# A hybrid DeltaNet, attention and Conformer trunk on one core: the solver's blocks in fewer stores and more loads, token buffers, and three orders of work

## The chip, the cores and the metric

The kernel runs on one core of one Trainium2 chip. The metric is the device time of one execution in microseconds, as the median of several runs: 1379.72 us for the kernel before, in three runs from 1378.24 to 1382.68 us. A core has five engines with an instruction stream each: TensorE (PE, with its weight loads as PEld), VectorE (DVE), ScalarE (ACT), GpSimd (POOL) and SyncE (SP). In this kernel SP issues nearly all transfers between memory (DRAM) and the on-chip buffers, so SP's stream is one queue of DMA issues.

## The reference

Two layers over 512 latent tokens of width 1024, with 256 context tokens, all in float32. Layer 0 mixes with gated DeltaNet heads in both directions and with attention; layer 1 with a Conformer convolution; a SwiGLU FFN stands behind each. Cut to what matters here:

```python
def reference(x, c, ctx, c_ctx, w_mod, ...):
    h, hc = x, ctx
    for layer in range(2):
        sh1, sc1, gt1, sh2, sc2, gt2 = ada_terms(c, w_mod[layer], b_mod[layer])   # silu(c) @ w_mod + b_mod
        a = rms_norm(h) * (1 + sc1) + sh1
        if layer == 0:
            ac = the same of hc with c_ctx
            y = hybrid_mixer(a, ac, ...)
        else:
            y = conformer_conv(a, ...)
        h = h + gt1 * rms_norm(y)
        f = swiglu_ffn(rms_norm(h) * (1 + sc2) + sh2, w_ffn_in[layer], w_ffn_out[layer])
        h = h + gt2 * rms_norm(f)
    return h

def gated_delta_chunked(q, k, v, g, beta, s0):           # 4 heads of 128, forward and reversed
    decay, kb = ...                                      # in chunks of tokens
    lower = where(strict, (kb @ k.T) * decay, 0)
    u, w = triangular_solve(lower + eye, [v * beta, kb * exp(gcum)])
    for each chunk:                                      # one after the other
        v_new = u - w @ state
        o = q_dec @ state + intra @ v_new
        state = state * exp(g_last) + k_tail.T @ v_new

def attend(q, k, v):                                     # 8 query heads, 2 key heads of 64, 768 keys
    return softmax(q @ k.T / 8) @ v
```

## The kernel before

A float32 product is made of three matmuls: each operand is split in a high and a low part (`whi`, `wlo`; `ah`, `al`), and high x high, high x low and low x high are added (lines 297 to 299, 204 to 206, 1760 to 1762). The split of a weight tile is a cast (`whi`, line 564) and a subtraction (`wlo`, line 573), mostly on DVE.

The program is written by a planner. `Plan.op` collects operations with their engines, costs, dependences and the buffers that they take; `Plan.run` is a list scheduler, which at each step takes from the ready operations the one with the smallest key: its start by the planner's own costs, less a weight times the sum of the longest path behind it and a bias by the operation's name, and, where there is a choice of engines, by its name and engine. The biases are tables of numbers: `BIAS0` for stage 0, `BIAS1` for stage 1, `BIAS` for stage 2, `BIAS2` for the tail. So a table sets both the order on each engine and which engine runs an operation. On the chip each engine works through its list in this order and waits on semaphores where an operand isn't there.

- **Stage 0** (`plan_inputs`). Six token tiles of 128x1024 (four of `xs`, two of `ctx`) are loaded into `xt` (`ld_x`, line 351), squared and summed on ACT (`x_sq`, line 355), brought to a root on POOL (line 180), scaled (`x_norm`, on ACT line 365 or DVE line 367) and transposed on PE (`ps_xt`, line 374) into `xnT`. Beside it the modulation is computed: sixteen weight tiles `mraw` (line 404) are multiplied with the conditioning on PE (`ps_mod`, line 411, four matmuls a tile), turned (line 426) and made into columns; the tokens are then modulated (`a`, line 446), cast to the high part (`aL` for the latent, `aC` for the context tokens) and subtracted to the low part (line 454). The first product of the tokens, keys and values of the attention (`ps_kv`, lines 297 to 299), needs all of these and the split weights `wkhi`, `wklo` (lines 338 and 342). The tiles `xt` have three buffers, `mraw` six.
- **Stage 1** (`plan_heads`). The DeltaNet projections with their short convolution, the gates, and `solver(d)` for the two directions d. The solver inverts the 32x32 unit triangles on the diagonals of the chunks, 4 blocks x 24 (6 chunks x 4 heads) of them, as 96 partitions of 32x32, in 31 steps of row operations on DVE. Its result and the transpose leave for DRAM in `x_out` (line 1110), into `xblk[d]`, from which they are read back in another layout.
- **Stage 2** (`plan_delta` and `plan_attention`). `inverse` builds the inverse of each chunk's triangle of 128 from the 32x32 blocks: `ld_xu` (line 1363) reads a chunk's blocks into `xu` (three buffers), `ld_off` (line 1371) the blocks off the diagonal into `m`, and a chain of small matmuls follows (`ps_w`, `ps_dx`, `ps_du`, line 1334), with copies on DVE, POOL and ACT between them. `step` then carries the state from chunk to chunk (`ps_xr`, `ps_p`, `ps_o`, `ps_ds`). `vt` and `ktl` (lines 1430 and 1444) are loads of values and keys for it. Attention has queries `ps_qt` (line 1213, from `qd`), scores `ps_sc` (lines 1241 and 1242), their exponentials `pr`, transposes `ps_pt` and products `ps_pv`. `ps_qtok` and `ps_qk` are transposed queries and query-key products for the DeltaNet output. Between them run the adaLN products of a later layer part: `wada` tiles of 128x1024 are loaded (line 1624) and multiplied on DVE (`a_dot`, line 1627).
- **Tail** (`plan_tail`). The output projection (`out_proj`, weights `whout`, product `ps_y`), ffn0 (weights `wfin`, product `ps_in`; then `wfout`, product `ps_y`), the Conformer, ffn1, and the rest of the 80 `wada` products. After each `out_proj` a residual is added to `hres`.

The two loops that the change rewrites are these: sixteen stores of 24 partitions in all (two directions, two orientations, four blocks), and twelve loads (two directions, six chunks) of 128 partitions.

```python
for b in range(4):
    SP.dma_start(xblk[d][w, 32 * b : 32 * b + 32].rearrange("r c h q -> (c h) r q"), t_[b * NB : (b + 1) * NB])
...
s["xu"] = scp.tile([P, 2, H, 32], F32, tag="xu", name="xu", bufs=3)
SP.dma_start(s["xu"], xblk[d][:, :, c].rearrange("w p h q -> p w h q"))
```

## Time and profile before

| what | value |
|---|---|
| median of the runs | 1379.72 us (1378.24 to 1382.68) |
| the profiled run, and its span | 1377.72 us, 1375.9 us |
| mean granted clock of PE | 0.992 |
| DMA | 184.76 MB, mean 134 GB/s |
| instructions in the span | 19258 |

The span reaches from the first to the last instruction of the profiled execution; all times of rows below are counted from its start. In a row of the timeline stand the start, the length, the engine, the line, the operation and the shapes, and in brackets the idle time ahead with what ended it. "SPq" is SP's queue of DMA issues: such a row's length is the time that the issue takes, not the transfer. The rows of the stages are shown in the prediction, where they are used.

### The profile page before, as it was taken

The numbers are of one execution on the slowest core, as the hardware profiler recorded it, in microseconds if no ns is written. First come the engines' busy times: TensorE is split into PE (matmuls) and PEld (weight loads), VectorE is DVE, ScalarE is ACT, GpSimd is POOL, SyncE is SP. The second block draws the span as 40 slices with busy tenths as digits, with TensorE's granted clock in tenths as the row PEclk, the third lists the DMA queues.
The fourth block names the chain that finished last, engine by engine and source line by source line (L and its number), as shares of the span: only waits on it lengthen the run. The fifth ranks groups of instructions, "written<-read, shape, count | busy, mean of one in ns | idle before, by whom it ended". The sixth has DMA issues, their size and how long they took to land.

```text
span 1375.9 us, 19258 instructions
## 1 busy us (share of the span) xinstructions
PE 1326.7 (96%) x7343; PEld 1116.3 (81%) x7343; DVE 857.8 (62%) x1625; ACT 453.4 (33%) x983; POOL 256.7 (19%) x347
## 2 busy tenths in 40 slices
PE   5999898999999999999999999999999999999998
PEld 4888797898877888888887878887798888888886
DVE  3588897888888666565667476649663334243223
ACT  6656534877524301111000142114342223222221
POOL 2668563411002300000000011323040000000000
PEclk9999998999999999999999999999999999999999
DMA  8445636641157464545557333201113223233231
GB/s 320 136 147 165 157 116 148 218 143 55 38 203 262 158 200 150 185 160 177 184 202 256 117 103 103 73 28 62 61 65 120 92 92 110 74 122 108 93 105 64
DMA packets 105900, 184.76 MB, mean 134 GB/s; under 512 B 33776, under 2 KB 50496, under 8 KB 105808
## 3 DMA queue, kind: packets, MB, share of 16 engines
q1 hardware_dynamic: 105808, 183.53, 41.3%
q8 instruction: 58, 0.95, 0.3%
q14 instruction: 34, 0.28, 0.1%
HBM read 172.45 MB, written 11.06 MB: 133 GB/s over the span
## 4 chain that ended last, share of the span: by engine, by line
PE 74%; DVE 12%; DMA 7%; issue 2%; ACT 2%; POOL 2%; SPq 1%; DVEq 0%; POOLq 0%; ACTq 0%
PE ps_in L204 12%; PE ps_in L206 12%; PE ps_in L205 12%; PE ps_y L1760 5%; PE ps_y L1762 5%; PE ps_y L1761 5%; DMA wada<-in_wmB 3%; PE ps_in L2114 2%; PE ps_in L2112 2%; PE ps_in L2113 2%; DVE wlo L573 2%; PE ps_pt L1271 2%; DVE cv L653 2%; DVE wada L1627 1%; PE ps_pv L1293 1%
## 5 line engine op out<-in xcount | busy, mean ns | idle before, releaser
L205 PE MATMUL ps_in<-al,whi 128*128 128x512 f32 (+1 forms) x768 | 285.7, 372 | 1.6 <-POOL al L573 1.6
L206 PE MATMUL ps_in<-ah,wlo 128*128 128x512 f32 (+1 forms) x768 | 285.5, 372 | 0.8 <-DVE wlo L573 0.8
L204 PE MATMUL ps_in<-ah,whi 128*128 128x512 f32 (+1 forms) x768 | 285.9, 372 | 0.0
L573 DVE TENSOR_TENSOR wlo<-wraw,whi 128x1024 fp32r<-128x1024 f32 x162 | 204.7, 1265 | 116.4 <-ACT whi L564 109.2
L204 PEld LDWEIGHTS ps_in<-ah,whi 128*128 128x128 f32 x768 | 144.6, 188 | 28.1 <-issue 2.3
L205 PEld LDWEIGHTS ps_in<-al,whi 128*128 128x128 f32 x768 | 144.6, 188 | 27.3 <-POOL al L573 2.3
L206 PEld LDWEIGHTS ps_in<-ah,wlo 128*128 128x128 f32 x768 | 144.6, 188 | 26.7 <-DVE wlo L573 2.1
L180 POOL TENSOR_TENSOR rr<-rr,mhalf 128x1 f32<-128x1 f32 x28 | 17.4, 624 | 790.6 <-DVE rr L1799 765.0
L564 DVE CAST whi<-wraw 128x1024 fp32r<-128x1024 f32 x93 | 64.8, 697 | 158.0 <-PE ps_in L205 108.6
L1760 PE MATMUL ps_y<-whi,hh 128*128 128x512 f32 x352 | 138.0, 392 | 1.8 <-DVE yg L1785 1.8
L1762 PE MATMUL ps_y<-wlo,hh 128*128 128x512 f32 x352 | 137.7, 391 | 0.0
L1761 PE MATMUL ps_y<-whi,hl 128*128 128x512 f32 x352 | 137.6, 391 | 0.0
L1965 ACT ACTIVATE sg<-ps_in 128x512 f32<-128x512 f32 x44 | 26.3, 598 | 302.9 <-PE ps_in L206 302.6
L564 ACT CAST whi<-wraw 128x1024 fp32r<-128x1024 f32 x69 | 72.3, 1049 | 122.7 <-PE ps_y L1761 70.5
L1627 DVE CUSTOM_DVE_ANT_0 wada<-wada,csrow 128x1024 f32<-128x1024 f32 x80 | 97.3, 1231 | 19.7 <-DMA wada<-in_wmB 19.4
L1760 PEld LDWEIGHTS ps_y<-whi,hh 128*128 128x128 f32 x352 | 66.2, 188 | 16.5 <-DVE yg L1785 2.2
L1762 PEld LDWEIGHTS ps_y<-wlo,hh 128*128 128x128 f32 x352 | 66.2, 188 | 14.5
L1761 PEld LDWEIGHTS ps_y<-whi,hl 128*128 128x128 f32 x352 | 66.2, 188 | 14.3
L1781 ACT ACTIVATE junk<-ps_y 128x512 bf16<-128x512 f32 x32 | 19.1, 598 | 137.5 <-PE ps_y L1762 121.0
L1968 DVE TENSOR_TENSOR sg<-sg,ps_in 128x512 f32<-128x512 f32 x44 | 29.1, 682 | 45.5 <-PE ps_in L206 45.5
L653 DVE SCALAR_TENSOR_TENSOR cv<-ps_in,convw,cv 128x510 f32<-128x510 f32 (+3 forms) x80 | 48.9, 639 | 2.6 <-ACT cv L568 1.1
L2112 PE MATMUL ps_in<-whi,ah 128*128 128x512 f32 x128 | 50.0, 391 | 0.0
(390 smaller groups left out, 2584.0 us busy)
## 6 DMA issues: line engine op xcount, KB each, us to landing
wraw<-in_wfin SPq DMA_DIRECT2D x88, 512.0 KB
wada<-in_wmB SPq DMA_DIRECT2D x80, 512.0 KB
wraw<-in_wfout SPq DMA_DIRECT2D x44, 512.0 KB
mraw<-in_wmA SPq DMA_DIRECT2D x16, 512.0 KB
wraw<-in_wcin SPq DMA_DIRECT2D x16, 512.0 KB
wraw<-in_wqkv SPq DMA_DIRECT2D x12, 512.0 KB
wraw<-in_wcout SPq DMA_DIRECT2D x8, 512.0 KB
rw<-grow SPq DMA_DIRECT2D x8, 384.0 KB
```

Source lines behind the costliest of these rows:

```text
L204: E.matmul(ps, wh, xh, start=start, stop=False)
L205: E.matmul(ps, wh, xl, start=False, stop=False)
L206: E.matmul(ps, wl, xh, start=False, stop=stop)
L564: {"ACT": S.copy, "DVE": V.tensor_copy, "Pool": G.tensor_copy}[e](dst, src)
L573: {"DVE": V, "Pool": G}[e].tensor_tensor(dst, a, b, o)
L653: V.scalar_tensor_tensor(s["cv"][:, o], s["ps"][:, i], convw[:, ft, j : j + 1], s["cv"][:, o], op0=ALU.mult, op1=ALU.add)
L1627: V.tensor_tensor_reduce(s["raw"], s["raw"], csrow[0], 1.0, 0.0, ALU.mult, ALU.add, accs[:, part, j : j + 1])
L1760: E.matmul(acc[t], ah[:, ts_], wh[:, o], start=i == 0 and j == 0, stop=False)
L1761: E.matmul(acc[t], al[:, ts_], wh[:, o], start=False, stop=False)
L1762: E.matmul(acc[t], ah[:, ts_], wl[:, o], start=False, stop=end)
L1968: V.tensor_tensor(s["g"], s["g"], pss[1]["ps"], ALU.mult)
L2112: E.matmul(acc[t], k["h"][:, tk], wh[:, o], start=False, stop=False)
```

## The change

Four things are changed.

1. `xt` gets five buffers in place of three and `mraw` four in place of six; the planner counts the first token load 2 us longer.
2. The tensor `xblk` in DRAM has the row within a block as its first dimension, then the block, the chunk and the head: [2, 32, 4, 6, H, 32] in place of [2, 128, 6, H, 32]. `x_out` stores a tile in one transfer of 96 partitions where it took four of 24: 4 stores in all in place of 16. The runs in memory are of 32 numbers (128 bytes) in both.
3. `ld_xu` reads a chunk in four transfers of 32 partitions, one for each block, in place of one of 128: 48 loads in all in place of 12. The planner's costs follow: 0.75 in place of 2.2 for a store of a tile, 4 x 0.47 in place of 0.47 for a load of a chunk.
4. The tables `BIAS0`, `BIAS` and `BIAS2` have new numbers throughout; `BIAS1` and the weights are the same. So stage 0, stage 2 and the tail are put in other orders, while stage 1 keeps its own up to `x_out`, save two small loads on SP that change places.

```diff
-BIAS0, TW0 = {'a_high': 75700, 'a_low': 206192, 'c_silu': -16514, ...
+BIAS0, TW0 = {'a_high': 4187, 'a_low': 281059, 'c_silu': 232311, ...
...
-    xblk = [drp.tile([2, P, 6, H, 32], F32, name=f"xblk{d}") for d in range(2)]
+    xblk = [drp.tile([2, 32, 4, 6, H, 32], F32, name=f"xblk{d}") for d in range(2)]
...
-                    s["x"] = sp.tile([P, D], F32, tag="xt", name="xt", bufs=3)
+                    s["x"] = sp.tile([P, D], F32, tag="xt", name="xt", bufs=5)
...
-                a = last["x"] = op({"SP": 1.47}, ld_x, seq=after("x"), lat=DLAT, take=("xt",))
+                a = last["x"] = op({"SP": 1.47}, ld_x, seq=after("x"), lat=DLAT if "x" in last else DLAT + 2, take=("xt",))
...
-                        w["raw"] = sp.tile([P, 1024], F32, tag="mraw", name="mraw", bufs=6)
+                        w["raw"] = sp.tile([P, 1024], F32, tag="mraw", name="mraw", bufs=4)
...
-        plan = Plan({"a": 6, "r": 2, "xt": 3, "mraw": 6, "wraw": 2, "w": 4, "rows": 2, "a32": 2, "wkr": 2}, BIAS0, TW0, SCALE0)
+        plan = Plan({"a": 6, "r": 2, "xt": 5, "mraw": 4, "wraw": 2, "w": 4, "rows": 2, "a32": 2, "wkr": 2}, BIAS0, TW0, SCALE0)
...
             def x_out(w):
                 def f():
                     t_ = s["xi"] if w == d else s["xj"]
-                    for b in range(4):
-                        SP.dma_start(xblk[d][w, 32 * b : 32 * b + 32].rearrange("r c h q -> (c h) r q"), t_[b * NB : (b + 1) * NB])
+                    SP.dma_start(xblk[d][w].rearrange("r b c h q -> (b c h) r q"), t_[0 : 4 * NB])
...
-            op({"SP": 2.2}, x_out(d), (a,), lat=DLAT)
-            op({"SP": 2.2}, x_out(1 - d), (b,), lat=DLAT)
+            op({"SP": 0.75}, x_out(d), (a,), lat=DLAT + 1)
+            op({"SP": 0.75}, x_out(1 - d), (b,), lat=DLAT + 1)
...
-                SP.dma_start(s["xu"], xblk[d][:, :, c].rearrange("w p h q -> p w h q"))
+                for b in range(4):
+                    SP.dma_start(s["xu"][32 * b : 32 * b + 32], xblk[d][:, :, b, c].rearrange("w r h q -> r w h q"))
...
-            lx = op({"SP": DMA}, ld_xu, seq=after("xu"), lat=DLAT, take=("xu",))
+            lx = op({"SP": 4 * DMA}, ld_xu, seq=after("xu"), lat=DLAT, take=("xu",))
```

Three places of the new order follow. The first is PE at the start of the program, up to the first product of the tokens (`ps_kv`). Before:

```order
L374 MATMUL ps_xt<-masks,xt 128x128 x24
L411 MATMUL ps_mod<-mraw,cz 32x256 x12
L426 MATMUL ps_mod<-quart,rows 128x2 x2
L374 MATMUL ps_xt<-masks,xt 128x128 x12
L411 MATMUL ps_mod<-mraw,cz 32x256 x4
L374 MATMUL ps_xt<-masks,xt 128x128 x4
L426 MATMUL ps_mod<-quart,rows 128x2 x2
L374 MATMUL ps_xt<-masks,xt 128x128 x8
L411 MATMUL ps_mod<-mraw,cz 32x256 x8
L297 MATMUL ps_kv_325<-wkhi,aL_101 128x272
```

With the change PE first has, three times, eight transposes `ps_xt` and four `ps_mod`, and then:

```order
L374 MATMUL ps_xt<-masks,xt 128x128 x8
L426 MATMUL ps_mod<-quart,rows 128x2 x2
L411 MATMUL ps_mod<-mraw,cz 32x256 x4
L374 MATMUL ps_xt<-masks,xt 128x128 x8
L426 MATMUL ps_mod<-quart,rows 128x2 x2
L411 MATMUL ps_mod<-mraw,cz 32x256 x4
L374 MATMUL ps_xt<-masks,xt 128x128 x4
L411 MATMUL ps_mod<-mraw,cz 32x256 x4
L374 MATMUL ps_xt<-masks,xt 128x128 x4
L411 MATMUL ps_mod<-mraw,cz 32x256 x4
L426 MATMUL ps_mod<-quart,rows 128x2 x2
L297 MATMUL ps_kv_333<-wkhi,aL_101 128x272
```

The modulation stands between the transposes in pieces of four, and 32 of its matmuls are ahead of the first `ps_kv`, where 24 were. On ACT the six norms (line 365) now stand between the squares, ahead of the cast `wkhi`; before, all six ran on DVE.

The second place is SP's queue at the border of stages 1 and 2 (`xblk_86` and `xblk_87` are the two directions; `zimg` is a store of the output gate, `csrow` a load). Before:

```order
L1110 DMA xblk_86<-xi 24x32x32 x4
L1142 DMA zimg<-zz 128x256
L1110 DMA xblk_86<-blk 24x32x32 x4
L1110 DMA xblk_87<-blk 24x32x32 x4
L1110 DMA xblk_87<-xi 24x32x32 x4
L1142 DMA zimg<-zz 128x256 x2
L1614 DMA csrow<-csd 128x1024
L1363 DMA xu<-xblk_86 128x2x128
L1363 DMA xu<-xblk_87 128x2x128
L1363 DMA xu<-xblk_86 128x2x128
L1430 DMA vt<-vimg 128x512 x2
L1371 DMA m_2894<-nimg_84 32x4x32 x2
```

With the change:

```order
L1109 DMA xblk_86<-xi 96x32x32
L1109 DMA xblk_86<-blk 96x32x32
L1141 DMA zimg<-zz 128x256
L1109 DMA xblk_87<-blk 96x32x32
L1109 DMA xblk_87<-xi 96x32x32
L1141 DMA zimg<-zz 128x256 x2
L1614 DMA csrow<-csd 128x1024
L1363 DMA xu<-xblk_86 32x2x128 x4
L1363 DMA xu<-xblk_87 32x2x128 x4
L1363 DMA xu<-xblk_86 32x2x128 x4
L1430 DMA vt<-vimg 128x512 x2
L1371 DMA m_2882<-nimg_84 32x4x32 x2
```

The stores are four rows of one transfer, and one of them has passed a `zimg`; the loads of the first three chunks are twelve transfers, in the place of three, ahead of the same `vt` and `m`.

The third place is PE at the first step of `inverse` (the first `ps_w` of each kernel). Before:

```order
L1561 MATMUL ps_qtok<-masks,qs 128x128 x8
L1213 MATMUL ps_qt<-masks,qd 128x128 x2
L1561 MATMUL ps_qtok<-masks,qs 128x128 x4
L1213 MATMUL ps_qt<-masks,qd 128x128 x2
L1334 MATMUL ps_w_3049<-xu,m_2894 64x32 x4
L1561 MATMUL ps_qtok<-masks,qs 128x128 x4
L1334 MATMUL ps_dx<-w_2898,u_2896 32x32 x4
```

With the change:

```order
L1561 MATMUL ps_qtok<-masks,qs 128x128 x4
L1212 MATMUL ps_qt<-masks,qd 128x128 x2
L1561 MATMUL ps_qtok<-masks,qs 128x128 x4
L1240 MATMUL ps_sc<-kst,qh 128x384
L1241 MATMUL ps_sc<-kst,ql 128x384
L1240 MATMUL ps_sc<-kst,qh 128x384
L1241 MATMUL ps_sc<-kst,ql 128x384
L1212 MATMUL ps_qt<-masks,qd 128x128 x6
L1333 MATMUL ps_w_3111<-xu,m_2882 64x32 x4
L1240 MATMUL ps_sc<-kst,qh 128x384
```

The last `ps_qtok` and four score matmuls, which stood behind the first steps of `inverse`, stand ahead of `ps_w`. In the rest of stage 2 attention's pieces are earlier and the steps of the delta chain later. In the tail, six `wada` in place of eight stand among the weights of the output projection, four in place of three go to every four tiles of `wfin`, and SP asks for the last of them with eighteen of ffn0's 22 tiles of `wfout` to come (nine in two lumps among the first four tiles), where eight were left before; the Conformer's matmuls are in another order.

More of the change, by code (lines that the diff above doesn't have):

```diff
@@ L132 @@
 XORD = (0, 1, 2, 3, 4, 5)
[L133 removed]
+BIAS0, TW0 = {'a_high': 4187, 'a_low': 281059, 'c_silu': 232311, 'c_tanh': 40826, 'col': 135122, 'e_ba': 126776, 'e_k': 155419, 'e_v': 228586, 'kv': -6027, 'ld_c': 85019, 'ld_k': -25467, 'ld_late': 33477, 'ld_m': -25475, 'ld_w': 11636, 'ld_x': -23852, 'mod': -40306, 'mods': 118753, 'quarters': 54203, 'rows': 81455, 'turn': -4629, 'w_high': 15179, 'w_low': -332635, 'x_copy': 85335, 'x_eps': 366451, 'x_norm': 27921, 'x_root': 1752, 'x_sq': 107381, 'x_turn': -5686, ('a_high', 'ACT'): 92650, ('a_high', 'DVE'): -546573, ('a_low', 'DVE'): 58817, ('a_low', 'Pool'): 146574, ('e_ba', 'ACT'): 62505, ('e_ba', 'DVE'): 63100, ('e_k', 'ACT'): 129098, ('e_k', 'DVE'): 46060, ('e_v', 'ACT'): -269350, ('e_v', 'DVE'): 12404, ('mod', 'ACT'): 25634, ('mod', 'DVE'): 33866, ('rows', 'ACT'): -100952, ('rows', 'DVE'): 250644, ('w_low', 'DVE'): 430085, ('w_low', 'Pool'): -182664, ('x_copy', 'ACT'): 3255, ('x_copy', 'DVE'): 8749, ('x_norm', 'ACT'): 180579, ('x_norm', 'DVE'): -196162}, 0.000200
```

5 lines of the change are left out of this document (2 added, 3 removed).

## The prediction

> **What bounds the kernel now.** I read the page's busy table and its chain first, then the same counts cut at the stages.
>
> ```profile
> PE 1326.7 (96%) x7343; PEld 1116.3 (81%) x7343; DVE 857.8 (62%) x1625; ACT 453.4 (33%) x983; POOL 256.7 (19%) x347
> PE 74%; DVE 12%; DMA 7%; issue 2%; ACT 2%; POOL 2%; SPq 1%; DVEq 0%; POOLq 0%; ACTq 0%
> ```
>
> PE is busy for 1326.7 of the span's 1375.9 us. The change leaves the matmuls as they are, so what it can win is the 49.2 us in which PE stands still, and time in which PE is busy at a low clock. In the table of windows (us of PE, PEld, DVE, ACT, POOL; then the granted clock, the DMA share, GB/s) the stages are:
>
> ```profile
> 10.00:60.00 50.00, 45.71 (x367) 36.74 (x368) 22.66 (x66) 35.76 (x71) 20.26 (x24) 0.93 0.70 254
> 60.00:226.00 166.00, 155.23 (x1029) 139.57 (x1029) 149.78 (x402) 84.55 (x221) 111.56 (x143) 1.00 0.54 140
> 226.00:394.00 168.00, 162.28 (x1436) 140.22 (x1434) 139.81 (x339) 114.75 (x320) 35.23 (x84) 0.96 0.38 118
> 394.00:700.00 306.00, 302.02 (x1412) 249.57 (x1413) 206.46 (x293) 50.55 (x101) 23.30 (x24) 1.00 0.56 188
> 700.00:1000.00 300.00, 292.56 (x1386) 242.36 (x1385) 197.63 (x348) 69.97 (x133) 46.51 (x46) 1.00 0.33 111
> 1000.00:1375.90 375.90, 368.94 (x1718) 307.86 (x1717) 140.22 (x173) 94.61 (x136) 19.14 (x24) 1.00 0.28 96
> ```
>
> The first 10 us hold no matmul. Between 10 and 60 PE loses 4.3 us, in stage 1 10.8 (DVE, at 149.78 of 166, is nearly as full as PE there), in stage 2 5.7, then 4.0, 7.4 and 7.0. The clock is below 1.00 in two stages only, the first and stage 2. So the gains to look for are the start, the border of stages 1 and 2, and small holes behind it.
>
> **Stage 0: five token buffers and a new order.** Rows of SP, of ACT and of PE, one group with its mean duration, and two pieces of the chain:
>
> ```profile
> 2.59 1.38 SPq L351 DMA_DIRECT2D xt<-in_xs  x3
> 12.92 0.33 SPq L351 DMA_DIRECT2D xt<-in_xs  x1
> 14.63 1.28 SPq L351 DMA_DIRECT2D xt<-in_ctx  x2
> ...
> 8.11 1.06 ACT L355 ACTIVATE sq<-xt 128x1024 bf16<-128x1024 f32 x1 [5.54 <-DMA xt<-in_xs]
> 9.07 0.19 ACT L355 ACTIVATION_READ_ACCUMULATOR sq<-xt 128x1 f32 x1
> 19.12 1.06 ACT L355 ACTIVATE sq<-xt 128x1024 bf16<-128x1024 f32 x1 [1.42 <-DMA xt<-in_ctx]
> 22.09 0.81 ACT L446 ACTIVATE a<-xnT,cols 128x512 f32<-128x512 f32 x1
> 22.94 0.62 ACT L314 CAST aL<-a 128x512 fp32r<-128x512 f32 x1
> 23.94 1.10 ACT L338 CAST wkhi<-wkr 128x1088 fp32r<-128x1088 f32 x1
> 25.20 0.58 ACT L314 COPY xnT<-ps_xt 128x512 f32<-128x512 f32 x1 [0.16 <-PE ps_xt L374]
> ...
> 28.88 0.39 PE L297 MATMUL ps_kv<-wkhi,aL 128*128 128x272 f32 x1
> L367 DVE TENSOR_SCALAR xt<-xt,ssq_in 128x1024 f32<-128x1024 f32 x6 | 4.5, 752 | 2.4 <-POOL ssq_in L180 2.3
> 20.54 0.56 POOL ssq_in L180
> 30.66 0.57 PE ps_mod L411 x8
> ```
>
> Before, the fourth token tile is asked for at 12.92, when a buffer is free, and the fifth and sixth at 14.63; the last but one reaches ACT at 19.12. With five buffers SP asks for five tiles in a row, so a fourth and fifth come behind the third at the pace of the first ones, and loading binds no more. What is late next is ACT: the order gives it all six norms, which ran on DVE at 752 ns each. The nearest row for such a pass on ACT is the square of the same 128x1024 tile, 1.06 us. ACT then has six squares of 1.06 + 0.19 and six norms of about 1.06, 13.9 us from 8.11 on, so to 22.0; the last norm waits for its root (0.56 on POOL, with DVE's step ahead of it about 1.1), to 23.1. Behind it stand, on ACT, wkhi 1.10, a copy 0.58, the modulation 0.81 and the cast 0.62: 26.2. So the first kv matmul (L297) can start at about 26.2 in place of 28.88, 2.7 us earlier, and two more groups of modulation matmuls are done by then, 2 x 0.57 = 1.1 us. Against this: PE works in shorter pieces from 11 to 26, and its clock, 0.93 in the mean of this stage before, may be low when the kv matmuls begin, or the smaller ring of four mraw buffers may hold modulation back. I take -2.3 us, from -3.8 (all of it) to +2.7 (the kv start gains nothing and 5.4 us of kv run at half clock). Stage 1 keeps its order and its loads (DMA share 0.54), so an earlier start passes through it.
>
> **The solver's blocks.** SP's rows, the last piece of the way out, the copy that makes the last tile, the return, and four windows:
>
> ```profile
> 207.52 3.02 SPq L1110 DMA_DIRECT2D xblk<-xi  x4
> 211.48 6.07 SPq L1110 DMA_DIRECT2D xblk<-blk  x8
> 217.65 3.10 SPq L1110 DMA_DIRECT2D xblk<-xi  x4
> 220.85 2.17 SPq L1142 DMA_DIRECT2D zimg<-zz  x2
> 223.55 2.08 SPq L1363 DMA_DIRECT2D xu<-xblk  x3
> 226.66 3.19 SPq L1371 DMA_DIRECT2D m<-nimg  x6
> ...
> 219.74 4.94 DMA xblk<-xi
> 212.04 1.05 ACT L564 COPY xi<-ps_x 96x512 f32<-96x512 f32 x2
> L1363 SPq DMA_DIRECT2D xu<-xblk x12: 360/374/464, 223.5 to 337.6; - x12
> 230.70 1.03 PE ps_w L1334 x8
> 236.80 0.32 PE ps_sc L1241
> ...
> 207.50:217.50 10.00, 10.00 (x74) 9.38 (x72) 8.19 (x17) 3.98 (x8) 4.23 (x12) 1.00 0.75 125
> 224.00:230.00 6.00, 2.60 (x17) 1.73 (x16) 5.01 (x15) 4.42 (x24) 2.30 (x8) 0.97 0.84 254
> 230.00:243.00 13.00, 12.30 (x90) 10.20 (x91) 7.15 (x17) 3.56 (x15) 2.29 (x9) 0.50 0.46 128
> 372.40:383.20 10.80, 10.50 (x110) 9.44 (x109) 7.77 (x15) 6.99 (x23) 0.84 (x1) 1.00 0.46 145
> ```
>
> The way out: sixteen transfers hold SP for 3.02 + 6.07 + 3.10 = 12.2 us; the last tile is ready at 213.1 and starts to leave at 217.65, because SP is behind; all has landed at 219.74 + 4.94 = 224.7. Four transfers take SP some 3 us at the 0.76 us of one such issue (6.07 / 8), so the last starts at 213.1. The bytes and the 128-byte runs stay the same in number. While these transfers run the DMA engines are busy for just 0.75: if that idle quarter is used, 17.2 us (207.5 to 224.7) become 12.9, and all lands at 220.4; if not, at 224.7 as before. I take 222, between the two, as nothing here shows a 96-partition transfer of such runs.
>
> The return: twelve loads become 48, 36 more issues at 0.374 us, 13.5 us of SP in all. Nine of these stand ahead of the first step, since three chunks' loads precede the vt and m loads, and each pushes them by about 0.4. If all has landed at 222: zimg (2.17) and csrow leave by 220.8, four pieces of the first chunk by 222.4, eight more by 225.7, two vt by 226.6, six m by 229.8. Before, the last m was issued by 226.66 + 3.19 = 229.85: what the way out wins the return spends, and the first ps_w stays at 230.7. If nothing lands earlier, it slips by 6 x 0.4 = 2.4 us. The other 27 extra issues fall on a queue with room between its loads and cost nothing unless a chunk's m or ktl loads come late.
>
> [...]
>
> What does help is the new order on PE. From 224 to 230 PE works 2.60 of 6 us. The change puts four score matmuls (0.32 us each at 236.80, at half clock: 1.3 us) and the last ps_qtok ahead of the first ps_w, some 2 us of work for that hole. I take -2.0 us for the border, with -3.4 (the whole hole) and +2.4 (the slip) as ends, the clock apart. The clock falls to 0.50 after this hole and stays there for 13 us with PE busy 12.30; half of that, 6.2 us, is its price. A hole half as long might spare it; I take it that it doesn't.
>
> [...]
>
> **The rest of stage 2 and the tail.** Attention is moved ahead and the delta steps back; PE is near full in 226 to 394, so I take 0, with 3 us to either side (half of its 5.7 us of holes). In the tail:
>
> ```profile
> 390.00:460.00 70.00, 64.37 (x334) 52.67 (x334) 59.31 (x94) 22.04 (x54) 17.52 (x19) 1.00 0.64 226
> 740.00:760.00 20.00, 18.17 (x81) 14.66 (x80) 15.31 (x23) 2.75 (x8) 0.00 (x0) 1.00 0.68 226
> 745.16 1.23 DVE L1627 CUSTOM_DVE_ANT_0 wada<-wada,csrow 128x1024 f32<-128x1024 f32 x1 [2.52 <-DMA wada<-in_wmB]
> ```
>
> At 745 DVE waits 2.52 us for a wada load, with the split of the next weights and the ps_y products queued behind it, and PE loses 1.83 of 20 us. The new order puts more wada products beside ffn0's wfin, where PE is dense, and has them all behind it when eighteen wfout tiles are left: -1.8 us, with +1.8 as the other end, since nine loads in two lumps ahead of the early wfout tiles can bring the same wait there. In 390 to 460 PE loses 5.6 us of 70 around out_proj; fewer wada there, -0.8 (0 to -2). The conformer's order is new on a DVE that fills a good part of that stage: 0, with 2 us to either side.
>
> **Sum.** -2.3 - 2.0 - 0.8 - 1.8 = -6.9 us. The profiled run took 1377.72, which makes 1370.8; the median shown is 1379.72, 2.0 us above it, so the forecast in its terms is **1372.8**. A measurement of this kernel tells about 0.3%, 4.1 us, from no change.
>
> **The rivals.**
>
> *The gains at the front go in waits.* Stage 1's DVE sets the pace, the kv phase starts cold, the blocks land no earlier. For it: DVE at 149.78 of 166, and the 2.4 us of the return. Against: ACT's sum, which frees 2.7 us. Only the tail's 1.8 us stay: 1377.9.
>
> *The clock holds.* With the holes at 11 to 26 and at 224 to 230 filled, neither low stretch comes: the forecast less 6.2 us and about 1 us of kv, 1365.6. For it: the hole's 3.4 us shrink to some 1.4. Against: all of ps_qt, ps_qtok and the scores hang on DVE's qd copies, and DVE is at 5.01 of 6 there.
>
> *Slower: the delta chain stands bare at the end of stage 2.* The return is late and attention goes first, so the last chunk's chain has nothing beside it. Its price: a chunk's chain, w to o, fills 372.4 to 383.2, 10.8 us with PE at 10.50, some 4 of them attention's; those become idle, and a hole of that kind brought 0.50 clock for 13 us, 6.2 more. That is +10.2 - 2.3 - 2.6 for stage 0 and the tail, with the border at 0: 1385.0. It decides when PE idles over 3 us in one piece before out_proj. Against: attention work still stands in the last rows of stage 2 in the new order.
>
> **How the numbers follow.** The forecast, 1368 to 1378, gets 0.50; the gains lost at the front 0.20; the clock that holds 0.15; the bare chain 0.15. Faster by over 0.3% is under 1375.6: all of the held clock and 0.42 of the forecast, 0.57. Within 0.3%: 0.08 of the forecast and the lost gains, 0.28. Slower: the bare chain, 0.15. The range leaves out the bare chain beyond its lower edge, some 0.12, and the deepest part of the held clock, 0.05: 1362 to 1384. The likeliest case's own is 1368 to 1378.
>
> **What would show it.** Right: the first ps_kv near 26.2 with six norms on ACT; the last block landing near 222, and the first ps_w within a us of where it stood relative to stage 1's end; a fuller PE in the 6 us ahead of it; no loss in wfout. Wrong: ps_kv not before 28.9; a clock of 0.50 in the kv matmuls, or none after the border; a hole over 3 us before out_proj; holes in the conformer beyond those of before.

## The result, and the profile after

| | median of 15 runs | range | profiled run | its span |
|---|---|---|---|---|
| before | 1377.67 us | 1371.0 to 1382.68 us | 1377.72 us | 1375.9 us |
| after | 1382.73 us | 1379.66 to 1387.49 us | 1384.46 us | 1382.7 us |

One run of the changed kernel, of 1459.26 us, and two of middle_new below, of 2934.78 and 3379.62 us, were disturbed and are left out. The changed kernel is slower: the ratio of its time to that of before is 1.0043, with a 95% interval of 1.0031 to 1.0054, so +5.9 us (4.3 to 7.4); the medians of the table differ by 5.1. The prediction was 1372.8 us with a range of 1362 to 1384; the time lies within the range, on the side that had a chance of 0.15.

The page of the changed kernel, its PE row and its chain by engine:

```profile
PE 1330.1 (96%) x7343; PEld 1115.2 (81%) x7343; DVE 866.6 (63%) x1634; ACT 448.9 (32%) x971; POOL 263.7 (19%) x350
...
PE 66%; DVE 16%; DMA 9%; ACT 3%; POOL 2%; issue 2%; SPq 1%; DVEq 0%; POOLq 0%; ACTq 0%
```

PE's share of the chain fell from 74% to 66%, DVE's rose from 12% to 16%: the chain to the end now runs over DVE more often. The windows of the same kernel (us of the window, then of PE, PEld, DVE, ACT, POOL; granted clock, DMA share, GB/s), with the edges used before, and three short ones:

```profile
10.00:60.00 50.00, 46.89 (x374) 36.41 (x375) 29.76 (x81) 30.69 (x61) 20.25 (x23) 1.00 0.72 254
60.00:226.00 166.00, 155.76 (x1025) 141.04 (x1023) 148.31 (x399) 84.04 (x217) 111.66 (x144) 0.98 0.53 142
226.00:394.00 168.00, 161.03 (x1433) 137.66 (x1432) 139.60 (x338) 116.69 (x325) 30.99 (x80) 0.98 0.41 123
394.00:700.00 306.00, 300.77 (x1403) 246.95 (x1403) 216.20 (x315) 50.80 (x101) 21.36 (x24) 1.00 0.62 202
700.00:1000.00 300.00, 290.43 (x1362) 239.61 (x1361) 185.98 (x313) 65.98 (x124) 58.88 (x50) 0.99 0.27 93
740.00:760.00 20.00, 20.00 (x90) 16.51 (x89) 10.06 (x12) 2.76 (x8) 0.00 (x0) 1.00 0.25 84
950.00:960.00 10.00, 6.14 (x34) 5.46 (x33) 9.99 (x20) 4.59 (x9) 4.69 (x2) 0.83 0.32 107
224.00:230.00 6.00, 3.95 (x25) 2.79 (x25) 5.81 (x19) 4.77 (x26) 1.15 (x4) 1.00 0.40 109
230.00:236.00 6.00, 4.27 (x37) 3.06 (x35) 4.71 (x12) 4.97 (x13) 4.44 (x7) 0.96 0.62 162
236.00:243.00 7.00, 7.00 (x42) 5.56 (x42) 2.79 (x6) 4.00 (x10) 1.18 (x5) 0.55 0.33 103
1000.00:1382.70 382.70, 375.20 (x1753) 313.47 (x1752) 145.03 (x184) 97.22 (x141) 19.81 (x26) 1.00 0.28 94
```

Between 10 and 60 the clock is 1.00 where it was 0.93, and PE does 1.2 us more work. From 700 to 1000 PE loses 9.6 us where it lost 7.4, and POOL's work there grew from 46.51 to 58.88 us. The worst ten microseconds are 950 to 960: PE at 6.14 of 10.

Fixed windows slide over the work when two kernels are shifted against each other. So I also cut each kernel's own trace at matmuls that all of them have. This table is worked out from the first and last start of such groups (us; kv is `ps_kv`, z `ps_z` of stage 1, w the first `ps_w`, mix the last product of stage 2, then the first product of the output projection, of ffn0's two products, and of the Conformer's input and output products):

```
               kv starts  to end of z   z to w  w to mix  projection  ffn0 in  ffn0 out  Conformer, in to out  out
before         28.9       27.6+160.4    13.8    160.6     49.7        250.9    124.9     134.1 (125.7+8.4)     52.2
after          27.5       27.4+160.9    16.4    158.7     49.8        252.2    124.5     139.0 (121.6+17.4)    52.1
tail_old       26.8       28.0+158.8    17.3    157.2     49.3        252.4    124.8     134.1 (125.6+8.5)     52.2
tail_new       29.3       28.5+160.8    13.6    159.2     50.5        253.8    123.7     138.8 (121.5+17.3)    52.2
stage0_new     26.7       28.7+159.9    13.9    162.3     51.1        254.2    124.9     134.1 (125.7+8.4)     52.4
wlo_dve2       26.7       30.8+160.6    17.6    156.1     50.4        253.4    125.3     133.6 (121.6+12.0)    53.5
wlo_dve8       26.9       27.9+158.6    17.6    157.7     49.5        254.2    123.9     130.5 (118.0+12.5)    54.6
blocks_new     27.4       27.6+159.1    15.5    161.8     49.5        252.3    127.1     134.1 (125.7+8.4)     52.3
middle_new     28.1       28.5+159.2    17.3    158.6     49.8        251.3    124.2     134.1 (125.7+8.4)     52.2
loads4_only    29.4       28.5+158.8    16.5    162.1     48.5        251.4    123.4     134.1 (125.6+8.5)     52.2
m_first        26.5       27.7+160.8    12.1    190.8     50.9        250.8    125.5     134.1 (125.6+8.5)     52.3
blocks_held    27.8       27.6+157.7    12.6    164.3     49.6        255.1    124.0     134.1 (125.6+8.5)     52.7
best_a         27.2       27.0+159.2    13.7    159.2     50.3        251.2    124.6     129.8 (122.7+7.1)     53.3
best_d         27.2       27.6+159.2    12.0    165.6     50.6        252.3    123.9     129.7 (122.6+7.1)     53.5
after_fix      26.5       28.3+159.4    17.2    159.1     51.5        254.3    124.8     130.8 (118.4+12.4)    54.8
```

The rows below the first two are the experiments (best_b and best_c are left out). The Conformer's column repeats to 0.1 us in kernels that share its code: 134.1 with the old table (seven rows besides before), 138.8 and 139.0 with the new one. Most other columns scatter by 2 to 4 us between profiled runs of the same code (ffn0 in: 250.8 to 255.1 with the old table). So a change of 4.9 us in the Conformer can be read from single profiles, and most of the rest needs the timed comparisons. Of these 4.9 us, the input products take 4.1 less, and the stretch from the last of them to the first output product takes 9.0 more (17.4 in place of 8.4).

**The Conformer.** The timeline of the changed kernel at its worst place, DVE, POOL and PE (`xtok` are the tokens that PE turns into `ps_a` for the next product):

```profile
948.95 6.02 DVE L2350 TENSOR_SCALAR xtok<-xtok,mv 128x512 f32<-128x512 f32 x4
...
949.86 4.83 POOL L573 TENSOR_TENSOR wlo<-wraw,whi 128x1024 fp32r<-128x1024 f32 x2
...
952.54 0.66 PE L1832 MATMUL ps_a<-masks,xtok 128*128 128x128 f32 x4 [2.02 <-DVE xtok L2350]
955.02 0.94 PE L1832 MATMUL ps_a<-masks,xtok 128*128 128x128 f32 x6 [1.83 <-DVE xtok L2350]
```

and the row of that tile, with least, median and greatest ns, of the changed kernel:

```profile
L2350 DVE TENSOR_SCALAR xtok<-xtok,mv x8: 537/542/2565, 948.9 to 969.8; 128x512 f32<-128x512 f32 x8
```

and of the kernel before:

```profile
L2350 DVE TENSOR_SCALAR xtok<-xtok,mv x8: 539/542/954, 945.6 to 964.8; 128x512 f32<-128x512 f32 x8
```

The same instruction takes 0.54 us alone and up to 2.57 us while POOL subtracts two weight tiles (`wlo`, 4.83 us for both) beside it. Four of them fill 6.02 us where four at 0.54 are 2.2, and PE stands still for 2.02 and 1.83 us in between. PE is also slower behind the second hole: the starts of thirteen of its 128x256 matmuls reach over 2.56 us, from 955.98 to 958.54, and over 1.41 (947.33 to 948.74) in wlo_dve8, an experiment below without these holes. In the trace of before the like was there, but PE waited less for it; its timeline has

```profile
931.27 2.78 DVE L573 TENSOR_TENSOR spl<-spa,sph 128x512 fp32r<-128x512 f32 x1
...
930.97 2.53 POOL L573 TENSOR_TENSOR wlo<-wraw,whi 128x1024 fp32r<-128x1024 f32 x1 [0.78 <-ACT whi L564]
```

where the same `spl` takes 0.68 us alone. What PE waited for these two tiles in the whole run (total, times, longest), before:

```profile
PE ps_y L2286 <- DVE spl L573: 1.4, 1, 1.4
PE ps_a L1832 <- DVE xtok L2350: 0.3, 1, 0.3
```

and in the changed kernel:

```profile
PE ps_a L1832 <- DVE xtok L2350: 3.9, 2, 2.0
PE ps_y L2286 <- DVE spl L573: 2.1, 3, 1.1
```

**The border of stages 1 and 2.** SP's rows of the changed kernel:

```profile
207.25 0.32 SPq L1109 DMA_DIRECT2D xblk<-xi  x1
207.67 2.90 SPq L1109 DMA_DIRECT2D xblk<-blk  x1
210.66 2.89 SPq L1141 DMA_DIRECT2D zimg<-zz  x1
213.64 0.38 SPq L1109 DMA_DIRECT2D xblk<-blk  x1
214.12 2.99 SPq L1109 DMA_DIRECT2D xblk<-xi  x1
217.20 3.35 SPq L1141 DMA_DIRECT2D zimg<-zz  x2
220.64 0.41 SPq L1614 DMA_DIRECT2D csrow<-csd  x1
221.14 6.46 SPq L1363 DMA_DIRECT2D xu<-xblk  x12
227.64 0.90 SPq L1430 DMA_DIRECT2D vt<-vimg  x2
228.59 3.20 SPq L1371 DMA_DIRECT2D m<-nimg  x6
```

The return starts 2.4 us earlier than before (221.14 against 223.55), but its first twelve issues take 6.46 us where three took 2.08, so `m` is issued by 231.79 where it was by 229.85, though stage 1 ended 1.1 us sooner. The blocks did land earlier: packets under 512 bytes, nearly all of them the blocks' runs of 128, pass at 440 to 620 in each half microsecond from 217.0 to 220.5 and have ended by 222.0; before, they passed at 390 to 550 up to 222.0, and the last landed at 224.7. The first `ps_w` comes 16.4 us behind stage 1 in place of 13.8. PE's rows ahead of it:

```profile
230.94 0.56 PE L1212 MATMUL ps_qt<-masks,qd 128*128 128x128 f32 x2 [0.36 <-POOL qd L564]
231.68 0.56 PE L1212 MATMUL ps_qt<-masks,qd 128*128 128x128 f32 x2 [0.18 <-POOL qd L564]
232.24 0.62 PE L1333 MATMUL ps_w<-xu,m 128*64 128x32 f32 x8
```

Here it follows `ps_qt` at once, with no wait for a transfer; before, it waited 1.1 us for `m`.

**Stage 0.** ACT and PE of the changed kernel:

```profile
19.83 1.06 ACT L355 ACTIVATE sq<-xt 128x1024 bf16<-128x1024 f32 x1 [1.20 <-DMA xt<-in_ctx]
21.83 1.15 ACT L365 ACTIVATE xt<-xt,ssq_in 128x1024 f32<-128x1024 f32 x1 [0.85 <-POOL ssq_in L180]
22.88 1.08 ACT L338 CAST wkhi<-wkr 128x1088 fp32r<-128x1088 f32 x1
...
25.24 0.62 ACT L314 CAST aL<-a 128x512 fp32r<-128x512 f32 x1
...
25.87 0.66 PE L374 MATMUL ps_xt<-masks,xt 128*128 128x128 f32 x4
26.45 0.64 PE L411 MATMUL ps_mod<-mraw,cz 128*32 128x256 f32 x8
27.02 0.61 PE L426 MATMUL ps_mod<-quart,rows 128*128 128x2 f32 x4
27.49 0.37 PE L297 MATMUL ps_kv<-wkhi,aL 128*128 128x272 f32 x1
```

The last norm ends at 22.98 (the sum had 23.1), though ACT waited 1.20 us for the last token tile, and the cast that `ps_kv` needs ends at 25.86 (26.2 in the sum). Then PE has transposes and modulation left ahead of `ps_kv`, until 27.49.

### The profile page after: what moved, and what is told of

The parts are those of the page before. It is cut to its first block, busy times and chain, and to the rows that moved or that the text cites. A ratio compares the mean times of both kernels' runs of the same rounds, so it can differ in the third digit from the quotient of the medians.

```text
span 1382.7 us, 19354 instructions
## 1 busy us (share of the span) xinstructions
PE 1330.1 (96%) x7343; PEld 1115.2 (81%) x7343; DVE 866.6 (63%) x1634; ACT 448.9 (32%) x971; POOL 263.7 (19%) x350
## 4 chain that ended last, share of the span: by engine, by line
PE 66%; DVE 16%; DMA 9%; ACT 3%; POOL 2%; issue 2%; SPq 1%; DVEq 0%; POOLq 0%; ACTq 0%
PE ps_in L206 9%; PE ps_in L204 9%; PE ps_in L205 9%; PE ps_y L1762 6%; PE ps_y L1760 6%; PE ps_y L1761 6%; DMA wada<-in_wmB 4%; DVE wlo L573 3%; DMA wraw<-in_wfin 2%; PE ps_in L2112 2%; PE ps_in L2114 2%; PE ps_in L2113 2%; DVE wada L1627 2%; DVE cv L653 1%; DVE whi L564 1%
## 5 line engine op out<-in xcount | busy, mean ns | idle before, releaser
L573 DVE TENSOR_TENSOR wlo<-wraw,whi 128x1024 fp32r<-128x1024 f32 x159 | 196.2, 1235 | 113.7 <-ACT whi L564 106.6
L573 POOL TENSOR_TENSOR matsl<-fraw,matsh 128x512 fp32r<-128x512 f32 x5 | 8.1, 1644 | 319.4 <-ACT matsh L564 319.4
L573 POOL TENSOR_TENSOR wlo<-wraw,whi 128x1024 fp32r<-128x1024 f32 x22 | 54.1, 2462 | 47.3 <-DVE whi L564 25.8
```

Of the source, the lines that this page charges most:

```text
L573: {"DVE": V, "Pool": G}[e].tensor_tensor(dst, a, b, o)
```

## The experiments

All fifteen were timed in up to five rounds, each beside the kernel before on the same chip, mostly twelve runs of each (eleven of tail_old, ten of middle_new, five of m_first, four of best_b and best_c); ratios are to it, with 95% intervals, and 0.1% is 1.4 us. The theory from this profile: the loss is the new order of the tail, by POOL's subtractions beside DVE's work in the Conformer. The rivals: the loss is the return of the blocks; or it is spread, and stage 0's gain was never there.

**tail_old.** The changed kernel with the tail's table of before.

```diff
-BIAS2, TW2 = (the table of after)
+BIAS2, TW2 = (the table of before)
```

> The changed kernel with the tail's table of before; stages 0 to 2 stay as changed. Theory A (the loss lies in the tail's new order, above all in the Conformer): from out_proj's start to the end it takes what it took before, so the span falls from 1382.7 to about 1376, and the time is that of the kernel before within 0.2%. Rival B (the loss comes from the front, from the blocks or attention's order): it stays within 1 us of the changed kernel, about 0.4% slower than before.

Ratio 0.9995 (0.9982 to 1.0007), median 1377.12 us. The loss is gone with the tail's table, and so is the pair of POOL's subtractions at 950: the Conformer takes 134.1 us.

**tail_new.** The reverse: the kernel before with the new tail's table alone.

```diff
-BIAS2, TW2 = (the table of before)
+BIAS2, TW2 = (the table of after)
```

> The kernel before with the tail's new table alone. Theory A: about 6 us slower than before (+0.4%), with 139 us in place of 134 from the first Conformer input product to the first output product. Rival B: within 1 us of before.

Ratio 1.0037 (1.0022 to 1.0052): +5.1 us (3.0 to 7.2), nearly all of the change's +5.9. The Conformer takes 138.8 us, 4.7 more. Its window from 880 to 960 against that of tail_old; tail_new first:

```profile
880.00:960.00 80.00, 73.87 (x387) 62.36 (x386) 56.79 (x93) 20.65 (x34) 29.94 (x21) 0.98 0.19 60
```

and tail_old:

```profile
880.00:960.00 80.00, 76.83 (x414) 65.50 (x413) 50.65 (x90) 21.69 (x38) 21.08 (x17) 1.00 0.16 53
```

The new order has 8.9 us more POOL work there and DVE is busy 6.1 us longer, for three instructions more; PE loses 3.0 us more and the clock dips to 0.98. (The Conformer begins 3.5 us later in tail_new, so the two windows aren't quite over the same work.)

**stage0_new.** The kernel before with the first stage of the change (five `xt`, four `mraw`, the first load counted longer, its table).

```diff
-s["x"] = sp.tile([P, D], F32, tag="xt", name="xt", bufs=3)
+s["x"] = sp.tile([P, D], F32, tag="xt", name="xt", bufs=5)
...
-w["raw"] = sp.tile([P, 1024], F32, tag="mraw", name="mraw", bufs=6)
+w["raw"] = sp.tile([P, 1024], F32, tag="mraw", name="mraw", bufs=4)
...
-BIAS0, TW0 = (the table of before)
+BIAS0, TW0 = (the table of after)
```

> The kernel before with stage 0's new table and buffers alone. If the 1.6 us by which the last ps_kv is earlier passes through stage 1 and 2, it is 1.5 us faster than before (0.1%); the prediction had 2.3. If stage 1 or the border takes it back, no change.

Ratio 0.9985 (0.9970 to 1.0000), so -2.1 us (-4.1 to 0.0), and `ps_kv` starts at 26.7. The gain is about there, though the interval touches one. The start of `ps_kv` scatters: 26.5 to 27.5 in the profiles of the table with the new stage 0, 26.5 to 29.4 in those with the old one.

**wlo_dve2.** The changed kernel with two of the Conformer's subtractions `wlo` emitted on DVE in place of POOL: the pair at 949.86, and nothing else. The order on all engines is otherwise kept.

```diff
+            conf = ph[0] == "2"
...
+                if conf and e == "Pool":
+                    n_low.append(e)
+                    if len(n_low) in (7, 8):
+                        e = "DVE"
                 tt_on(e, s["l"], s["raw"], f32(s["h"]), ALU.subtract)
```

> The changed kernel with two operations moved: the two subtractions of the Conformer's output weights (wlo, 128x1024) that ran on POOL at 949.9 to 954.7 stand on DVE behind the four scalings xtok and the splits of a. Theory C (POOL's work beside them stretched the four xtok from 2.2 to 6.0 us, and PE waited 3.9 us for them): the four xtok take 2.2 us again, PE's two holes before ps_a go, and the span falls by 2 to 3 us, as the subtractions now take 2.4 us of DVE ahead of the first output products. Rival D (the order leaves too little PE work beside this chain, whoever runs the subtractions): the holes stay or move behind the splits, and the span changes by less than 1 us.

Ratio 1.0014 (1.0000 to 1.0027), so 0.29% or 4.0 us less than the change (some 1.5 to 6.5 by the two intervals). The tile's row and the window of this kernel (its lines are seven further down):

```profile
L2357 DVE TENSOR_SCALAR xtok<-xtok,mv x8: 539/541/546, 952.4 to 969.5; 128x512 f32<-128x512 f32 x8
```

```profile
950.00:960.00 10.00, 9.90 (x73) 8.95 (x71) 9.47 (x30) 7.80 (x13) 1.42 (x2) 1.00 0.04 14
```

No `xtok` is above 0.55 us, PE works 9.90 of 10, and the stretch ahead of the output products falls from 17.4 to 12.0 us, while those products take 1.4 longer: -5.4 + 1.4 = -4.0. DVE took over work from POOL and the kernel got faster: it is the overlap that costs, not the amount of DVE work.

**wlo_dve8.** All eight of the Conformer's POOL subtractions on DVE.

```diff
-                    if len(n_low) in (7, 8):
+                    if len(n_low) in (1, 2, 3, 4, 5, 6, 7, 8):
```

> The changed kernel with all eight of the Conformer's wlo subtractions that were planned on POOL put on DVE where they were issued. Theory C (POOL's work beside DVE's stretches DVE): beside what the last two gave (4 us), the three holes of 2.1 us at 883 to 899 go, at a cost of six times 1.2 us of DVE where DVE has room; from the first Conformer input product to the first output product it takes 131 to 133 us, against 139 of the changed kernel and 133.6 with two moved. Rival D (DVE's load is what counts): more than 134 us.

Ratio 1.0007 (0.9991 to 1.0024), the Conformer 130.5 us and its output products 54.6. Against wlo_dve2 that is 3.1 us less in the one and 1.1 more in the other, and the ratio is 0.0007 or 1.0 us lower; by the intervals the six others aren't told from nothing.

**blocks_new.** The kernel before with the new layout, the stores and the loads alone; the planner's costs and all tables as before, so that the order stays.

```diff
-for b in range(4):
-    SP.dma_start(xblk[d][w, 32 * b : 32 * b + 32].rearrange("r c h q -> (c h) r q"), t_[b * NB : (b + 1) * NB])
+SP.dma_start(xblk[d][w].rearrange("r b c h q -> (b c h) r q"), t_[0 : 4 * NB])
...
-SP.dma_start(s["xu"], xblk[d][:, :, c].rearrange("w p h q -> p w h q"))
+for b in range(4):
+    SP.dma_start(s["xu"][32 * b : 32 * b + 32], xblk[d][:, :, b, c].rearrange("w r h q -> r w h q"))
```

> The kernel before with the new layout of xblk alone: four stores of 96 partitions, 48 loads of 32, with the planner's costs and all tables of before, so that nothing else changes its place. Theory E (what the merged stores win, the nine more load issues ahead of vt and m spend, and more): from the last ps_z to the first ps_w it takes 16 to 17 us in place of 13.8, and since PE has less to do there in the old order, the time rises by 1 to 3 us (0.1 to 0.2%). Rival F (the stores' earlier landing carries): 13 us or less, and 1 to 2 us faster.

Ratio 1.0024 (1.0009 to 1.0038): +3.3 us. In its waits of PE (total, times, longest) stands

```profile
PE ps_w L1333 <- DMA m<-nimg: 4.1, 1, 4.1
```

where before had one wait of 1.1 us: the first step waits for `m`, which stands behind the return's issues, and comes 15.5 us behind stage 1 (16 to 17 were expected).

**middle_new.** The same with the planner's new costs and the new table of stage 2.

```diff
+op({"SP": 0.75}, x_out(d), (a,), lat=DLAT + 1)
...
+lx = op({"SP": 4 * DMA}, ld_xu, seq=after("xu"), lat=DLAT, take=("xu",))
...
+BIAS, TW = (the table of after)
```

> The kernel before with the blocks' layout, their planner costs and stage 2's new table; stage 0 and the tail as before. The prediction had -2.0 us for this. From the sum of the runs so far (old tail -0.7, stage 0 alone -2.1) it should be 1 us slower than before (+0.1%): ps_w 2.5 us later, made up by the scores ahead of it, and nothing gained. If attention's order is worth its -2.0, 1376.5.

Ratio 1.0013 (0.9996 to 1.0031): +1.8 us. Attention's new order may win back 1.5 of the blocks' 3.3; the intervals overlap, so that isn't shown. The three parts alone add up to -2.1 + 1.8 + 5.1 = +4.8, beside +5.9 (4.3 to 7.4) together: they don't depend on each other in a way that can be seen.

**loads4_only.** The kernel before with the old layout and its sixteen stores, but four loads a chunk.

```diff
-SP.dma_start(s["xu"], xblk[d][:, :, c].rearrange("w p h q -> p w h q"))
+for b in range(4):
+    SP.dma_start(s["xu"][32 * b : 32 * b + 32], xblk[d][:, 32 * b : 32 * b + 32, c].rearrange("w r h q -> r w h q"))
```

> The kernel before with the loads of a chunk in four pieces of 32 partitions (48 loads), and with the stores, the layout and all tables of before. Theory E (the loads' issues on SP, nine more ahead of the first m, make the border late): the stores end as before, the first ps_w comes 3.5 to 4 us later than before after the last ps_z (17 to 18 us in place of 13.8), and the kernel is 3 to 5 us slower. Rival G (what the blocks alone lost, 3.3 us, came from the stores or the new layout): within 1 us of before.

Ratio 1.0036 (1.0024 to 1.0048): +5.0 us for the loads alone, so the new stores may win some 1.7 (5.0 - 3.3), which the intervals don't tell from nothing. Three of its rows on SP:

```profile
223.08 5.61 SPq L1364 DMA_DIRECT2D xu<-xblk  x12
228.74 0.90 SPq L1431 DMA_DIRECT2D vt<-vimg  x2
229.68 3.19 SPq L1372 DMA_DIRECT2D m<-nimg  x6
```

The twelve issues take 3.5 us more than the three of before, and `m` is out by 232.87, 3.0 later. The first `ps_w` moved by 2.7, and waits 4.4 us for `m`.

**m_first.** blocks_new with the loads of `m` ahead of the blocks' loads, by a dependence in the planner.

```diff
-lx = op({"SP": DMA}, ld_xu, seq=after("xu"), lat=DLAT, take=("xu",))
 l1 = op({"SP": 2 * DMA}, ld_off(m1, 32), after(("m1", d)), lat=DLAT)
 l2 = op({"SP": DMA}, ld_off(m2, 64), after(("m2", d)), lat=DLAT)
+lx = op({"SP": DMA}, ld_xu, seq=after("xu") + ((l1, l2) if i == 0 else ()), lat=DLAT, take=("xu",))
```

> The blocks alone (stores of 96 partitions, 48 loads) on the kernel before, with the loads of m for the first chunk of each direction asked for ahead of that chunk's blocks; the planner puts both vt there too, and sets some of stage 2 anew behind it. Theory E: m no longer waits behind twelve issues; the first ps_w comes 11 to 13 us after the last ps_z, in place of 15.5 with the blocks alone and 13.8 before, and the 3.3 us that the blocks alone lost are won back, 0 to 2 us under before. Rival G: first ps_w and time as with the blocks alone, 0.2% slower.

Ratio 1.0205 (1.0187 to 1.0224). The first `ps_w` came 12.1 us behind stage 1, 3.4 sooner than in blocks_new, but the rest of stage 2 took 190.8 us in place of 161.8: with one dependence more, the list scheduler laid the whole stage in another order. This tells nothing of the loads.

**best_b and best_c.** The same dependence, with stage 0 of the change and all of the Conformer's subtractions on DVE; best_b has the new blocks, best_c the old ones. The lines beside those of wlo_dve8 and stage0_new are:

```diff
+lx = op({"SP": DMA}, ld_xu, seq=after("xu") + ((l1, l2) if i == 0 else ()), lat=DLAT, take=("xu",))
```

> Stage 0's new table and buffers, the Conformer's subtractions on DVE, the blocks' new layout and the m loads ahead of it, all on the kernel before with its tables for stage 2 and the tail. If the parts add up: 3.7 us of the first two and 0 to 2 of the last, 1372 to 1374, 0.3 to 0.4% under before. If m ahead of the loads gives nothing, about 1377.

> As the one before, but with the blocks' layout, stores and loads of before: m ahead of three loads in place of twelve. By theory E the first m is issued 1.2 us earlier at most, and the blocks land as late as before (the last store started at 217.65), so the border is the same within 1 us: 1373 to 1375, 0.25% under before. If this is faster than the one with the new layout, the new layout has no use even with m ahead.

Ratios 1.0160 (1.0139 to 1.0181) and 1.0182 (1.0158 to 1.0207): the same spoilt order (191.1 and 188.3 us from the first `ps_w` to the end of stage 2), so no answer.

**blocks_held.** blocks_new with the planner left alone, and only SP's issues shifted as they are written out: the loads of the third chunk and both `vt` are held back until the first `m` are out.

```diff
+                def out(t=s["xu"]):
                     for b in range(4):
-                        SP.dma_start(s["xu"][32 * b : 32 * b + 32], xblk[d][:, :, b, c].rearrange("w r h q -> r w h q"))
+                        SP.dma_start(t[32 * b : 32 * b + 32], xblk[d][:, :, b, c].rearrange("w r h q -> r w h q"))
+                seen[0] += 1
+                held.append(out) if seen[0] in (3,) else out()
...
+                    seen[1] += 1
+                    while seen[1] >= 4 and held:
+                        held.pop(0)()
...
+                held.append(out) if seen[1] < 4 else out()
```

> The blocks alone (stores of 96 partitions, 48 loads) on the kernel before; on SP the six m loads now stand behind the first two chunks' loads, and the third chunk's four loads and both vt behind them. All other engines keep the order of the blocks alone. Theory E: the first m is issued 2.7 us earlier, the first ps_w comes 12 to 13 us after the last ps_z (15.5 with the blocks alone, 13.8 before), and the time falls by 2 to 4 us, to that of before within 1 us. Rival G (the layout or the stores cost the time): 15 us and 0.2% slower, as with the blocks alone.

Ratio 0.9990 (0.9975 to 1.0004); the interval lies below that of blocks_new. SP's rows:

```profile
219.45 3.68 SPq L1365 DMA_DIRECT2D xu<-xblk  x8
223.17 3.18 SPq L1376 DMA_DIRECT2D m<-nimg  x6
226.39 2.02 SPq L1365 DMA_DIRECT2D xu<-xblk  x4
```

`m` is out at 226.35, and the first `ps_w` comes 12.6 us behind stage 1. So the loss of blocks_new, in the old order of PE, was the queue ahead of `m`. Even then the new blocks don't gain measurably over before. The two profiles alone wouldn't have shown the difference: from stage 1's end to the end of stage 2 they have 176.9 and 177.3 us, and in that of blocks_held the clock was at half from 224 to 243.

**best_a.** The kernel before with stage 0 of the change, as in stage0_new, and all of the Conformer's POOL subtractions (five in this order) on DVE.

```diff
+BIAS0, TW0 = (the table of after)
...
+                if conf and e == "Pool":
+                    n_low.append(e)
+                    if len(n_low) in (1, 2, 3, 4, 5, 6, 7, 8, 9, 10, 11, 12, 13, 14, 15, 16, 17, 18, 19):
+                        e = "DVE"
```

> The kernel before with stage 0's new table and buffers, and with the Conformer's five wlo subtractions that ran on POOL put on DVE where they were issued. Stage 0 gives 2.1 us. In the Conformer of before DVE's spl took 2.8 us where 0.7 is usual, beside two such subtractions (931 to 936), and PE lost 1.4 us to it: by theory C 1 to 2 us more, about 1375 in all; by rival D no more than stage 0's 2.1 us, or less, since DVE is full there.

Ratio 0.9973 (0.9958 to 0.9989), median 1376.02 us: 3.7 us faster than before (1.5 to 5.8). The Conformer takes 129.8 us in place of 134.1 and its output products 53.3 in place of 52.2.

**best_d.** best_a with the blocks of blocks_held.

```diff
+held.append(out) if seen[0] in (3,) else out()
```

> Stage 0's new table and buffers, the Conformer's subtractions on DVE, and the blocks with m ahead as in blocks_held, with the tables of before for stage 2 and the tail. If the parts add: 3.7 us and what blocks_held shows, so 1373 to 1375, 0.25 to 0.4% under before.

Ratio 0.9973 (0.9955 to 0.9990): no better than best_a, so the new blocks add nothing that these runs can tell where `m` isn't held up.

**after_fix.** The changed kernel with wlo_dve8 and SP's order of blocks_held.

```diff
+                    if len(n_low) in (1, 2, 3, 4, 5, 6, 7, 8):
...
+held.append(out) if seen[0] in (3,) else out()
```

> The changed kernel with both causes taken away: the Conformer's eight subtractions of POOL on DVE, and on SP the first m loads ahead of the third chunk's loads and of vt. The first alone gave 1.0007 of before. If the queue on SP is the rest: the first ps_w 13 to 14 us after the last ps_z in place of 16.4, and 1 to 3 us less, 0.998 to 1.000 of before. If not: 1.0007 again.

Ratio 0.9996 (0.9978 to 1.0014), beside 1.0007 for wlo_dve8. The intervals overlap, and the first `ps_w` stays 17.2 us behind stage 1, where 13 to 14 were expected: in the new order of PE the score matmuls and `ps_qt` stand ahead of it, and an earlier `m` finds PE still at these.

## Why the prediction was wrong, step by step

| step | predicted | measured |
|---|---|---|
| stage 0 | -2.3 (-3.8 to +2.7) | -2.1 (-4.1 to 0.0) alone |
| border and rest of stage 2 | -2.0 (-3.4 to +2.4), and 0 ± 3 | +1.8 (-0.6 to +4.3) alone |
| tail: projection, `wada`, Conformer | -0.8, -1.8, 0 ± 2 | +5.1 (3.0 to 7.2) alone |
| sum | -6.9 | +5.9 (4.3 to 7.4) |

**The step that failed first is the Conformer's, "0, with 2 us to either side".** It was +4.9 in the profile. I had looked at DVE's mean load there and at nothing that stood beside it, so that "holes in the conformer" stood among the signs of being wrong while the sum put them at nothing. The price was in the trace of before: a subtraction of 0.68 us on DVE took 2.78 beside POOL's, and PE waited 1.4 us for it. With that row, the question for the new order would have been where POOL's subtractions fall, and whether PE waits for the DVE work beside them. wlo_dve2 shows the cause: with the one pair moved, 4.0 of the 5.9 us came back. The rows show the size: 0.54 us became 2.57, longer by 2.03, beside POOL instructions of 2.42 us each (4.83 for the two). What inside the chip stretches such an instruction, no run here tells; that the overlap with POOL's subtractions is what costs, wlo_dve2 shows.

**The border went to its other end.** The prediction had the first `ps_w` stay where it was, or slip by 2.4 "if nothing lands earlier". The blocks landed by 222.0, as taken, and it slipped by 2.6 all the same. Two prices were off. The stores were to hold SP for 3 us; they held it 0.32 + 2.90 + 0.38 + 2.99 = 6.6, since two of the four issues took 2.9 us each, and a `zimg` between them another 2.89. And twelve loads took 6.46 us, 0.54 apiece, where I had put 0.4 (0.46 and 0.47 in blocks_new and loads4_only). The 2.4 is also added up wrongly: nine issues are named and six counted, and loads4_only has the nine at 3.5 us. In the old order of PE the mechanism, issues ahead of `m`, is shown by loads4_only (+5.0 us) and by blocks_held, where the loss goes. In the changed kernel it isn't what held `ps_w`: there PE comes to it without a wait, and with `m` issued earlier (after_fix) it stays at 17.2 us. The score matmuls and `ps_qt`, taken as work that fills a hole, stand in its way.

**The hole was half filled, and it didn't pay.** PE works 3.95 of the 6 us from 224, where it worked 2.60: 1.35 more, where some 2 us had been put. From 230 to 236 it works 4.27 us where it worked 5.30. The half clock that I took to stay was shorter: 0.96 and 0.55 in the two windows from 230 to 243, where both had 0.50, which is 0.04 x 6 + 0.45 x 7 = 3.4 us lost in place of 6.5. So a part of the rival "the clock holds" came true in this profile. It isn't shown to be the change: tail_new, with stages 0 to 2 of before, had 0.50 and 0.74 there, and the mean clock over all runs is 0.9895 for middle_new and 0.9898 for the kernel before beside it. Nothing of it is left in the time of stage 2: from stage 1's end to the last product of stage 2 the changed kernel takes 175.1 us, and the kernel before 174.4.

**Stage 0 was right in mechanism and, within the interval, in size.** The chain over ACT came out as added up, 25.86 for 26.2; `ps_kv` started at 27.49, since PE's own rows ahead of it, which I had not added up, ran until then. The "two more groups of modulation" are one: the rows of the new order hold 28 of its matmuls ahead of `ps_kv`, not 32, where 24 were, so its 1.1 us is 0.6 and the lower end -3.3. And loading still bound a little: ACT waited 1.20 us for the sixth tile, which SP asked for at 13.46. With an interval 2 us wide to either side, that -2.1 lies so near -2.3 is luck. The cold kv phase that I allowed for, 5.4 us at half clock by a guess that no row gave, didn't come: the clock was 1.00 from 27.49 to 54.90.

**The `wada` terms brought little.** The hole at 740 is gone (20.00 of 20, from 18.17), as forecast; ffn0's output phase fell by just 0.4 us (124.9 to 124.5; 1.2 in tail_new), so that most of the 1.8 was lost again in the same phase. The 0.8 at the projection did not come: 49.8 against 49.7 us. On their own these are within the scatter of the profiles.

**The slower rival got the side but not the cause.** It gave 1385.0, near the time measured, by a bare chain at the end of stage 2. That chain did not stand bare: the delta part from the first `ps_w` on was 1.9 us shorter than before, and PE's longest wait from 330 to 394 was 2.2 us, under the 3 us that were to decide it, a length that I chose and no trace gave. Its closeness is chance, and that the time lies within the range is chance too: the range reaches up to 1384 only because it takes in the lower edge of this rival.

**The base was 2 us too high.** The 1372.8 adds 2.0 us to the profiled run for a median of three runs; over fifteen the median is 1377.67, that of the profiled run. The sum of -6.9 doesn't depend on it.

What stays open: whether the new order of attention gains 1.5 us over the old one, and whether the other six subtractions are worth anything.

## What to carry to other kernels

Before trusting a new order, list the instructions that took several times their usual length in the old trace and what ran on POOL beside them: that price moves with the order, and it counts where PE waits for DVE (here four `xtok` took 6.02 us in place of 2.2, and PE waited 3.9 us for them). A subtraction that POOL takes off DVE can cost more than it saves: two of them moved back were worth 4 us here. Issues on one queue are a cost of what stands behind them: four loads for one cost 5 us here where an urgent load followed, and where it didn't (blocks_held at 0.9990 of before, best_d beside best_a at 0.9973 both) they won nothing that could be measured. And work moved ahead of a step to fill its wait can become what the step waits for: in after_fix the first `ps_w` stayed 17.2 us behind stage 1.
